# Four expert blocks move from dense matmuls to row gathers in a one-core decoder step

## The chip, the cores and the metric

The kernel runs on one core of one Trainium2 chip. A time is device microseconds of one execution of the whole program. Times of the kernel before, three runs: 3084.05, 3080.38 and 3078.86 us, so a median of 3080.38 us.

## The reference

The program is one layer of a decoder trunk for 512 prompt tokens and 64 sample tokens, with a model width of 2048. A modulation, a combined input projection, two recurrent and convolutional head groups and an output projection come first; they are not touched here. Then comes a mixture of 16384 single-neuron experts (cut to what matters):

```python
q = (xb @ w_q).reshape(PEER_BLOCK, PEER_HEADS, 2, HALF_DIM)          # 8 heads, two halves
sc = jnp.einsum('thpk,pnk->thpn', q, sub_keys)                       # 128 keys in each half
v1, i1 = lax.top_k(sc[:, :, 0], 16)
v2, i2 = lax.top_k(sc[:, :, 1], 16)
...                                                                  # top 16 of the sums
eidx = i1 * 128 + i2                                                 # 128 picks a token
g = softmax(top)
act = gelu(einsum('td,thkd->thk', xb, expert_u[eidx])) * g
out = einsum('thk,thkd->td', act, expert_v[eidx])
x = x + gate2 * out ;  y = rmsnorm(x, final_g)
```

So each token picks 128 of the 16384 experts, takes the product of its 2048-wide row with each picked row of `expert_u`, and sums the picked rows of `expert_v` with the results as weights.

## The kernel before, in words

The 16384 experts are 128 blocks of 128, a block being all experts with the same first key. At run time the kernel counts how often each first key is picked and sorts the blocks by it. The first `L` blocks (80) are computed **densely**: every prompt token against all 128 experts of the block on TensorE, in three matmuls per product (high and low parts of the fp32 operands), and the result is multiplied with a matrix of weights that is zero where nothing was picked. The picks of prompt tokens that fall in the other 48 blocks, and all picks of the sample tokens, are **gathered**: an indirect DMA issued by GpSimd brings up to 128 rows of 2048 floats (one for each partition, 1.05 MB if all are there), and VectorE takes the dot product (line 1577) or adds the scaled row to a sum (line 1605). One such gather is a **slot**. Prompt tokens are sorted by how many picks they have outside the dense blocks, and cut into five groups. `SORTED` gives for each group its first token, its size and its number of slots; in the two groups of 64 tokens a token has two partitions, so its room is twice the slots. The numbers of slots are fixed when the program is built; a partition with no pick left brings no row, but VectorE works through the whole slot all the same. If a token had more picks than room, a slow second path at the end of the program would run.

The sample tokens (slot group 0) have 64 slots, the five prompt groups have 37, 23, 40, 33 and 26, together 159. Each slot is used twice, once for u and once for v.

The stages that matter, in order of time:

- until 1127 us: projections, heads, queries and scores.
- **The U stage**, 1127 to 2120 us: 160 pieces. A piece is half a dense block of `expert_u`: SP loads 512 KB (`raw`), ScalarE makes its high part (`xhi`, line 1203), GpSimd its low part (`xlo`, line 1204), and TensorE runs 24 matmuls (line 1713). Two pieces end in an activation (`act`, line 1716) that goes to DRAM (`actd`). Between the pieces VectorE chooses and sorts, later builds the weight matrix (`op` and `wr`, line 1922; small matmuls on line 1936; `gd` in DRAM), and uses the u slots. Gathers go into a ring of five row buffers here, and at most four are fetched ahead.
- **The V stage**, 2120 to 3053 us: 80 steps of two pieces each. A step multiplies four dense blocks with a quarter of the 2048 columns: 48 matmuls (line 1736). The blocks are taken in groups of eight (two steps for each quarter) and at the end of four; after each group's quarter VectorE adds the four banks to `acc` (line 1765). For each four blocks, GpSimd loads the activations (`actr`) and the weights (`gsb`) back, VectorE multiplies them (`weigh`) and ScalarE and VectorE split the product (`halve`: `ahi` on line 1683, `alo` on line 1687). The v slots run beside it, with seven row buffers; their order is group 0, 3, 1, 2, 4, 5. The sum of a finished group is scattered to DRAM (`accd`).
- the end: the last group of dense blocks, the scattered sums added by TensorE (`tok`), the sample tokens' own finish (`finish_b`), the final norm and the stores of `y`.

Each engine runs its instructions in the order in which the program issues them, and that order is written out by hand. In the U stage a loop over pieces decides before each piece how many slots to use: at fixed rates while the slots are still being chosen, and after the last choice evenly over the pieces that are left, so that at the end of the stage all u slots and the first ten v slots have been used (`gather_to` with `NU + EARLY_V`, `E0 = NU2 - 14`). The weight matrix is spread over the pieces up to `E0 - 6`. In the V stage a table of room per step sets when each slot is used. On GpSimd one queue holds the `xlo` of the dense pieces, the gathers, the loads of `actr` and `gsb`, the stores of `gd` and the scatters. A gather waits there until its row buffer has been used by VectorE, and everything behind it waits too.

Of the kernel before, what the change touches and what calls it, by code (L numbers as in the profile page):

```python
# [33 lines left out]
L = 80  # L34
SG = 4
GROUPS = (8,) * 9 + (4, 4)
# [5 lines left out]
SORTED = ((0, 64, 37), (64, 64, 23), (128, 128, 40), (256, 128, 33), (384, 128, 26))  # L42
# [40 lines left out]
def build(ctx, tc, A, O, dbg=None):  # L83
# [1503 lines left out]
    def gather_v(i):  # L1587
# [7 lines left out]
        def add(j):  # L1595
# [22 lines left out]
            for o in range(0, 128, n):  # L1618
                after.append([gu[0] + 2 + 4 * (o > 0), lambda o=o: out(o)])
            after.append([gu[0] + 2 + 4 * (128 // n), lambda: row_log.__setitem__(a, True)])  # L1620
# [57 lines left out]
    def halve(sg, part):  # L1678

        if part == 0:  # L1680
            pool = ep if sg % 3 < 2 else pools["vx"]
            hi, lo = (pool.tile([128, SG, NA], F32R, name=f"{x}{sg}", tag=f"{x}{sg % 3}", bufs=1) for x in ("ahi", "alo"))
            S.activation(hi, acts[sg], AF.Copy)
            ahg[sg] = (hi, lo)
            return
        hi, lo = ahg[sg]
        V.tensor_sub(lo, acts.pop(sg), r32(hi))  # L1687
        for j in range(SG):
            ahl[SG * sg + j] = (hi[:, j, :], lo[:, j, :])
# [101 lines left out]
    def token_norm(sq, n, nm, pool, banks):  # L1791
# [12 lines left out]
        if nm == "a":  # L1804
            V.tensor_copy(R, pr[:, :n])
        else:
            S.activation(R, pr[:, :n], AF.Copy)
# [131 lines left out]
    def g_out(b, pg):  # L1939
# [5 lines left out]
        if b0 == TC // 4 - 1:  # L1945
            full = stg.pop(c)
            for q in range(0, L, L // 4):
                puts.append(lambda q=q: G.dma_start(
                    gd[q // SG:(q + L // 4) // SG, :, c, :].rearrange("s p x -> p s x"),
                    full[:, q:q + L // 4, :].rearrange("p (s i) t -> p s (i t)", i=SG)))  # L1950
# [31 lines left out]
    for n in range(NU2):  # L1982
# [61 lines left out]
        if n - E0 == 2:  # L2044
            load_group(0)
        for sg, o in ((0, 3), (1, 7)):
            if n - E0 == o:
                load_weights(sg)
        if n - E0 == 6:
            weigh(0)  # L2050
        if n - E0 == 7:
            halve(0, 0)
        if n - E0 == 8:
# [4 lines left out]
        if n == NU2 - 1:  # L2058
            weigh_kept(2)
    hp_.close()  # L2060
# [13 lines left out]
    jobs[0] = [lambda: weigh_kept(3)]  # L2074
    jobs[1] = [lambda: halve(1, 0)]
    jobs[2] = [lambda: halve(1, 1)]
    for sg in range(2, L // SG):
# [7 lines left out]
        jobs.setdefault(h_, []).append(lambda sg=sg: halve(sg, 0))  # L2085
        jobs.setdefault(h_ + 2, []).append(lambda sg=sg: halve(sg, 1))
# [206 lines left out]
```

## Time and profile before

| what | value |
|---|---|
| median of three runs | 3080.38 us |
| the profiled execution | 3082.9 us, span 3081.0 us |
| granted TensorE clock, mean over the span | 0.987 |
| U stage, first to last of its matmuls | 1127.4 to 2120.1 us |
| V stage, first to last of its dense matmuls | 2120.1 to 3052.7 us |
| TensorE, VectorE, ScalarE, GpSimd busy | 97%, 72%, 34%, 57% |
| DMA, mean over the span | 286 GB/s |

The share of busy time of TensorE counts each matmul from its start to its modelled end, and matmuls overlap. The rows of windows therefore give a number in brackets behind the busy time, which is how many instructions fall into the window; the time between two starts is read from it. In a window's row the last three numbers are the granted clock, the mean busy share of the 16 DMA engines, and the GB/s that they moved.

### The profile page before, as it was taken

To read this page: it belongs to the slowest core of one execution; us is meant where nothing else is said; L and a number is where in the kernel's file an instruction comes from. 1 tells how busy PE (TensorE), PEld (TensorE's weight loads), DVE (VectorE), ACT (ScalarE), POOL (GpSimd) and SP (SyncE) were. 2 spreads that over 40 slices of the span, in tenths; PEclk is the share of its full clock that TensorE was granted. 3 is DMA by queue.
4 is the path that set the end of the run, shared out by engine and by line. 5 is a ranking of instruction groups with operands and counts; after the bars stand their busy time and mean duration, and the time that the engine had idled before them with its cause. 6 is when DMAs were issued, how large, how long until landed. Compare 5 with 4: busy or idle time off the path is not lost. (4 is left out here: it accounts for less than half of the span.)

```text
span 3081.0 us, 49243 instructions
## 1 busy us (share of the span) xinstructions
PE 2985.7 (97%) x18521; PEld 2546.5 (83%) x18521; DVE 2222.8 (72%) x3422; ACT 1051.4 (34%) x1675; POOL 1757.3 (57%) x1071
## 2 busy tenths in 40 slices
PE   6999999999999999999999999999999999989996
PEld 4788888899999998878888888877888878878775
DVE  6465532153366899988899999867788798798875
ACT  3344311232253232224655655532322222222222
POOL 2233333344313336666677777777787787876851
PEclk9999999999999999999999999999999999999998
DMA  9743566644432238999879999999999998999973
GB/s 400 295 153 135 177 217 212 212 163 146 132 120 91 74 99 291 315 350 382 318 285 396 384 407 358 383 379 382 377 409 411 410 373 299 361 373 395 382 261 131
DMA packets 238901, 880.90 MB, mean 286 GB/s; under 512 B 36246, under 2 KB 37142, under 8 KB 178102
## 3 DMA queue, kind: packets, MB, share of 16 engines
q0 software_dynamic: 78096, 475.29, 38.8%
q1 hardware_dynamic: 148896, 381.17, 35.0%
q10 hardware_dynamic: 11664, 21.24, 1.8%
q8 instruction: 146, 2.39, 0.3%
q14 instruction: 99, 0.81, 0.1%
HBM read 878.84 MB, written 65.76 MB: 307 GB/s over the span
## 5 line engine op out<-in xcount | busy, mean ns | idle before, releaser
L1204 POOL TENSOR_TENSOR xlo<-raw,xhi 128x1024 fp32r<-128x1024 f32 x320 | 800.4, 2510 | 273.2 <-ACT xhi L1203 270.1
L1203 ACT ACTIVATE xhi<-raw 128x1024 fp32r<-128x1024 f32 x320 | 338.4, 1061 | 789.1 <-PE pv L1736 365.1
L1577 DVE SCALAR_TENSOR_TENSOR u<-u,hT 128x2048 f32<-128x2048 f32 x223 | 504.4, 2282 | 99.0 <-DMA u<-u,rows 98.7
L1605 DVE SCALAR_TENSOR_TENSOR accB<-v,dots,accB 128x2048 f32<-128x2048 f32 x211 | 496.2, 2352 | 108.1 <-DMA v<-v,rows 106.0
L1736 PE MATMUL pv<-ahi,xhi 128*128 128x512 f32 x1280 | 504.6, 394 | 18.1 <-ACT xhi L1203 12.5
L1713 PE MATMUL pu<-hhi,xhi 128*128 128x512 f32 x1280 | 507.0, 396 | 0.7 <-ACT qt L1229 0.7
L1736 PE MATMUL pv<-alo,xhi 128*128 128x512 f32 x1280 | 502.5, 393 | 2.3 <-DVE alo L1687 2.3
L1713 PE MATMUL pu<-hhi,xlo 128*128 128x512 f32 x1280 | 499.0, 390 | 5.7 <-POOL xlo L1204 5.7
L1736 PE MATMUL pv<-ahi,xlo 128*128 128x512 f32 x1280 | 502.0, 392 | 0.0
L1713 PE MATMUL pu<-hlo,xhi 128*128 128x512 f32 x1280 | 499.4, 390 | 0.0
L1549 POOL DMA_INDIRECT u<-u,rows x223 | 226.8, 1017 | 166.2 <-DVE u L1577 124.1
L1736 PEld LDWEIGHTS pv<-ahi,xhi 128*128 128x128 f32 x1280 | 243.1, 190 | 73.0 <-ACT xhi L1203 15.6
L1713 PEld LDWEIGHTS pu<-hhi,xlo 128*128 128x128 f32 x1280 | 240.7, 188 | 57.4 <-POOL xlo L1204 6.6
L1713 PEld LDWEIGHTS pu<-hhi,xhi 128*128 128x128 f32 x1280 | 240.6, 188 | 56.4 <-issue 1.7
L1736 PEld LDWEIGHTS pv<-alo,xhi 128*128 128x128 f32 x1280 | 243.0, 190 | 52.7 <-DVE alo L1687 2.6
L1736 PEld LDWEIGHTS pv<-ahi,xlo 128*128 128x128 f32 x1280 | 242.8, 190 | 51.2 <-POOL xlo L1204 0.2
L1713 PEld LDWEIGHTS pu<-hlo,xhi 128*128 128x128 f32 x1280 | 240.7, 188 | 47.3
L1549 POOL DMA_INDIRECT v<-v,rows x223 | 244.5, 1096 | 60.5 <-issue 39.1
L873 POOL TENSOR_TENSOR wlo_q<-raw_q,whi_q 128x1024 fp32r<-128x1024 f32 x30 | 73.3, 2443 | 175.3 <-ACT whi_q L872 113.4
L1930 ACT ACTIVATE op<-op,it 128x128 f32<-128x128 f32 x512 | 155.2, 389 | 0.0
L1716 ACT ACTIVATE act<-pu 128x512 f32<-128x512 f32 x80 | 47.9, 599 | 297.9 <-PE pu L1713 285.6
L138 POOL TENSOR_TENSOR wlo_o<-raw_o,whi_o 128x1024 fp32r<-128x1024 f32 x31 | 75.1, 2423 | 112.0 <-ACT whi_o L136 108.5
(570 smaller groups left out, 5610.4 us busy)
## 6 DMA issues: line engine op xcount, KB each, us to landing
wa<-w_ada SPq DMA_DIRECT2D x96, 1024.0 KB, 7.2
raw<-ut SPq DMA_DIRECT2D x160, 512.0 KB, 7.8
raw<-vq SPq DMA_DIRECT2D x320, 256.0 KB, 14.9
gd<-stg POOLq DMA_DIRECT2D x64, 320.0 KB, 12.0
gsb<-gd POOLq DMA_DIRECT2D x20, 1024.0 KB, 11.4
actd<-act ACTq DMA_DIRECT2D x76, 256.0 KB, 7.8
actr<-actd POOLq DMA_DIRECT2D x19, 1024.0 KB, 12.0
raw_o<-w_out SPq DMA_DIRECT2D x32, 512.0 KB, 3.7
```

Of the source, the lines that this page charges most:

```text
L138: lo_engine(share).tensor_sub(lo, raw, r32(hi))
L873: G.tensor_sub(lo, qraw.pop(j), r32(hi))
L1203: S.activation(hi, raw, AF.Copy)
L1204: G.tensor_sub(lo, raw, r32(hi))
L1549: G.indirect_dma_start(out=out, out_offset=None, in_=src, in_offset=bass.IndirectOffsetOnAxis(ap=idx, axis=0), bounds_check=NE * 128 - 1, ...
L1577: V.scalar_tensor_tensor(r, r, 1.0, st["h"], op0=ALU.mult, op1=ALU.mult, accum_out=dots[i][:, j:j + 1])
L1605: V.scalar_tensor_tensor(st["a"], r, dots[i][:, j:j + 1], st["a"], op0=ALU.mult, op1=ALU.add)
L1713: PE.matmul(pu, st[:, kk, :], movA[mv](k), start=k == 0 and a == 0, stop=k == KD - 1 and a == 2)
L1716: S.activation(act, pu, AF.Gelu_apprx_tanh)
L1736: PE.matmul(pv, st, mv, start=first and j == 0 and a == 0, stop=last and not (end and k >= LATE_K) and j == SG - 1 and a == 2)
L1930: S.activation(ops[:, j0 + j, :], ops[:, j0 + j, :], AF.Copy, scale=it[2][:, b * 4 + j:b * 4 + j + 1])
```

## The change

`L` becomes 76: four blocks of 128 experts fewer are computed densely, so the U stage has 152 pieces, and the V stage 76 steps, with one group of four blocks at its end in place of two. The picks that fell into those four blocks are now gathered. The slots become 36, 25, 44, 36 and 29, together 170. The store of the weight matrix is cut into parts of 20 blocks, the last part being smaller. The other edits move work or give it to another engine:

- the scatter of a finished group is issued two uses of a slot later, and its buffer is released one use later;
- the second group of four blocks is split in two parts (`halve(1, ..)`): the first three blocks are split from their own call, the first half of it before the V stage begins;
- the first loads of `actr` and `gsb`, their product and their split move three to four pieces later behind `E0`; in the V stage the split of each later group moves one or two quarter steps later;
- the six points at which the sample tokens' finish goes on (`fplan`) are spread over the last steps in another way;
- the copy of the final norm's factors goes from VectorE to ScalarE, and three of the last stores of `y` go from SP's queue to ScalarE's.

```diff
-L = 80
+L = 76
-GROUPS = (8,) * 9 + (4, 4)
+GROUPS = (8,) * 9 + (4,)
-SORTED = ((0, 64, 37), (64, 64, 23), (128, 128, 40), (256, 128, 33), (384, 128, 26))
+SORTED = ((0, 64, 36), (64, 64, 25), (128, 128, 44), (256, 128, 36), (384, 128, 29))
...
-                after.append([gu[0] + 2 + 4 * (o > 0), lambda o=o: out(o)])
-            after.append([gu[0] + 2 + 4 * (128 // n), lambda: row_log.__setitem__(a, True)])
+                after.append([gu[0] + 4 + 4 * (o > 0), lambda o=o: out(o)])
+            after.append([gu[0] + 3 + 4 * (128 // n), lambda: row_log.__setitem__(a, True)])
...
-    def halve(sg, part):
+    def halve(sg, part, a=0, b=SG):
+        if sg not in ahg:
+            pool = ep if sg % 3 < 2 else pools["vx"]
+            ahg[sg] = [pool.tile([128, SG, NA], F32R, name=f"{x}{sg}", tag=f"{x}{sg % 3}", bufs=1) for x in ("ahi", "alo")]
+        hi, lo = (x[:, a:b, :] for x in ahg[sg])
...
+            S.activation(hi, acts[sg][:, a:b, :], AF.Copy)
...
+        V.tensor_sub(lo, acts[sg][:, a:b, :], r32(hi))
...
-        if nm == "a":
-            V.tensor_copy(R, pr[:, :n])
-        else:
-            S.activation(R, pr[:, :n], AF.Copy)
+        S.activation(R, pr[:, :n], AF.Copy)
...
-        if n - E0 == 2:
+        if n - E0 == 5:
             load_group(0)
-        for sg, o in ((0, 3), (1, 7)):
+        for sg, o in ((0, 5), (1, 10)):
             if n - E0 == o:
                 load_weights(sg)
-        if n - E0 == 6:
+        if n - E0 == 8:
             weigh(0)
-        if n - E0 == 7:
+        if n - E0 == 10:
             halve(0, 0)
-        if n - E0 == 8:
+        if n - E0 == 11:
             halve(0, 1)
...
             weigh_kept(2)
+            halve(1, 0, 0, 3)
...
-    jobs[0] = [lambda: weigh_kept(3)]
-    jobs[1] = [lambda: halve(1, 0)]
-    jobs[2] = [lambda: halve(1, 1)]
+    jobs[0] = [lambda: weigh_kept(3), lambda: halve(1, 1, 0, 3)]
+    jobs[1] = [lambda: halve(1, 0, 3)]
+    jobs[2] = [lambda: halve(1, 1, 3)]
...
-        jobs.setdefault(h_, []).append(lambda sg=sg: halve(sg, 0))
-        jobs.setdefault(h_ + 2, []).append(lambda sg=sg: halve(sg, 1))
+        jobs.setdefault(h_ + 2, []).append(lambda sg=sg: halve(sg, 0))
+        jobs.setdefault(h_ + 3, []).append(lambda sg=sg: halve(sg, 1))
...
-    fplan = {(last, 3), (last + 1, 0), (last + 1, 2), (last + 2, 0), (last + 2, 1), (last + 2, 3)}
+    fplan = {(last, 1), (last + 1, 1), (last + 1, 3), (last + 2, 0), (last + 2, 2), (last + 3, 0)}
...
-            nc.sync.dma_start(O["y"][:, k, :NA], ak)
+            (nc.scalar if order.index(k) in (3, 8, 12) else nc.sync).dma_start(O["y"][:, k, :NA], ak)
```

Two places show how this moves the instructions. The first is GpSimd's queue in the last twenty pieces of the U stage. A row `xlo` is one dense piece, `u_N` is the gather of u slot N of a group, `h2r` fetches a group's token rows, and `gd` stores a part of the weight matrix. Before:

```order
L1204 TENSOR_TENSOR xlo_20265<-raw_20190,xhi_20264 128x1024
L1948 DMA gd<-stg_19883 128x5x128
L1549 DMA u_4_20297<-u,rows_9005 128x2048
L1549 DMA u_5_20302<-u,rows_9005 128x2048
L1204 TENSOR_TENSOR xlo_20340<-raw_20259,xhi_20339 128x1024
```

With the change:

```order
L1204 TENSOR_TENSOR xlo_20201<-raw_20118,xhi_20200 128x1024
L1549 DMA u_29_20223<-u,rows_9003 128x2048
L1549 DMA u_30_20228<-u,rows_9003 128x2048
L1549 DMA u_31_20233<-u,rows_9003 128x2048
L1549 DMA u_32_20238<-u,rows_9003 128x2048
L1204 TENSOR_TENSOR xlo_20276<-raw_20195,xhi_20275 128x1024
L1946 DMA gd<-stg_20019 128x5x128
L1549 DMA u_33_20280<-u,rows_9003 128x2048
L1549 DMA u_34_20285<-u,rows_9003 128x2048
L1549 DMA u_35_20290<-u,rows_9003 128x2048
L1558 DMA h2r_20295<-h2d,tok 128x2048
L1204 TENSOR_TENSOR xlo_20329<-raw_20270,xhi_20328 128x1024
```

Where two gathers stood between two dense pieces, three or four stand now. Counted over the last twenty pieces of the stage (from one `xlo` to the next), 34 row fetches were issued before and 59 are issued now; in the pieces ahead of the last twenty-four the counts per ten pieces are the same to within four.

The second place is the same queue in the V stage, in the middle of the sample tokens' slots. A `v_N` is the gather of a v slot, and two `xlo` in a row are one step. Before:

```order
L1204 TENSOR_TENSOR xlo_22387<-raw_22121,xhi_22386 128x1024
L1204 TENSOR_TENSOR xlo_22391<-raw_22207,xhi_22390 128x1024
L1549 DMA v_41_22425<-v,rows_8995 128x2048
L1660 DMA gsb_22433<-gd 128x2048
L1549 DMA v_42_22461<-v,rows_8995 128x2048
L1204 TENSOR_TENSOR xlo_22481<-raw_22216,xhi_22480 128x1024
L1204 TENSOR_TENSOR xlo_22485<-raw_22295,xhi_22484 128x1024
```

With the change:

```order
L1204 TENSOR_TENSOR xlo_22180<-raw_21913,xhi_22179 128x1024
L1204 TENSOR_TENSOR xlo_22184<-raw_22000,xhi_22183 128x1024
L1549 DMA v_43_22205<-v,rows_8995 128x2048
L1549 DMA v_44_22223<-v,rows_8995 128x2048
L1660 DMA gsb_22228<-gd 128x2048
L1549 DMA v_45_22256<-v,rows_8995 128x2048
L1204 TENSOR_TENSOR xlo_22278<-raw_22009,xhi_22277 128x1024
L1204 TENSOR_TENSOR xlo_22282<-raw_22093,xhi_22281 128x1024
```

Between two steps two or three gathers stood, 11 for each four steps; now there are three, 12 for each four steps in full slots, and up to 15 where the slots of a group run empty.

More of the change, by code (lines that the diff above doesn't have):

```diff
@@ L1676, in weigh_kept @@
                         g[:, :, j * TC:(j + 1) * TC], op=ALU.mult)
-    def halve(sg, part):
+    def halve(sg, part, a=0, b=SG):
[3 more added lines that the diff above has]
+        hi, lo = (x[:, a:b, :] for x in ahg[sg])
         if part == 0:
[L1681 to L1684, printed above, removed]
+            S.activation(hi, acts[sg][:, a:b, :], AF.Copy)
             return
[L1686 to L1689, printed above, removed]
+        V.tensor_sub(lo, acts[sg][:, a:b, :], r32(hi))
+        for j in range(a, b):
+            ahl[SG * sg + j] = (hi[:, j - a, :], lo[:, j - a, :])
     ahg = {}
@@ L1946, in g_out @@
             full = stg.pop(c)
[L1947 to L1950, printed above, removed]
+            for q in range(0, L, 20):
+                e = min(q + 20, L)
+                puts.append(lambda q=q, e=e: G.dma_start(
+                    gd[q // SG:e // SG, :, c, :].rearrange("s p x -> p s x"),
+                    full[:, q:e, :].rearrange("p (s i) t -> p s (i t)", i=SG)))
     def put(n):
```

## The prediction

> **What bounds the kernel now.** I read the page's shares first, then the V stage in windows, then who waited for whom.
>
> ```profile
> PE 2985.7 (97%) x18521; PEld 2546.5 (83%) x18521; DVE 2222.8 (72%) x3422; ACT 1051.4 (34%) x1675; POOL 1757.3 (57%) x1071
> L1736 PE MATMUL pv<-ahi,xhi 128*128 128x512 f32 x1280 | 504.6, 394 | 18.1 <-ACT xhi L1203 12.5
> 1900.00:2000.00 100.00, 100.00 (x723) 81.33 (x722) 85.24 (x79) 59.58 (x133) 75.67 (x56) 1.00 0.98 391
> 2200.00:2300.00 100.00, 100.00 (x443) 82.84 (x442) 80.30 (x45) 27.40 (x26) 79.64 (x49) 1.00 1.02 410
> 2300.00:2400.00 100.00, 100.00 (x443) 82.84 (x442) 84.29 (x49) 23.82 (x23) 79.79 (x50) 1.00 1.02 411
> 2500.00:2600.00 100.00, 95.61 (x410) 78.06 (x409) 89.93 (x52) 20.48 (x18) 76.41 (x49) 0.97 0.91 339
> 2700.00:2800.00 100.00, 91.80 (x398) 75.28 (x397) 85.92 (x50) 23.46 (x21) 75.11 (x48) 0.97 0.98 380
> ```
>
> TensorE is busy, but its mean of 394 ns is not its pace: in the window from 2200 us 443 matmuls start in 100 us, one each 0.226 us. A block costs 96 matmuls (48 for u, 48 for v), so 21.7 us of TensorE and not the 38 us that 394 ns would give. The same windows show the second limit: DMA at a share of 1.02 and 410 to 411 GB/s while TensorE runs without a gap. Both are full there. Where TensorE does lose time, it waits for what DMA brings late:
>
> ```profile
> PE pv L1736 <- ACT xhi L1203: 12.5, 3, 6.9
> PE pu L1713 <- POOL xlo L1204: 5.7, 2, 3.5
> PE ph L1823 <- DMA tokb<-accs: 4.3, 1, 4.3
> PE pv L1736 <- DVE alo L1687: 2.3, 1, 2.3
> PE ph L1802 <- DVE rcfb L159: 2.3, 1, 2.3
> PE pv L1736 <- ACT ahi L1683: 1.6, 1, 1.6
> DVE accB L1605 <- DMA v<-v,rows: 100.1, 66, 5.0
> POOL u L1549 <- DVE u L1577: 108.7, 74, 4.6
> ```
>
> The first six rows are TensorE's own waits. The last two, VectorE's from 2120 to 3000 us and GpSimd's from 1400 to 2120 us, are the reserve: 100 us of waiting for v rows and 109 us for a free row buffer, little of which reached TensorE. So the kernel runs at TensorE's pace with DMA just able to follow, and the change takes from the first and gives to the second.
>
> **What the change removes.** 4 blocks x 96 matmuls x 0.226 us = 86.8 us of TensorE, 43.4 in each stage. The small matmuls of the weight matrix stay in number. DMA loses, with the sizes of these rows, 4 x (2 x 0.524 + 4 x 0.262) = 8.4 MB of dense rows and about 4 MB of `actd`, `actr`, `gd` and `gsb`:
>
> ```profile
> raw<-ut SPq DMA_DIRECT2D x160, 512.0 KB, 7.8
> raw<-vq SPq DMA_DIRECT2D x320, 256.0 KB, 14.9
> actd<-act ACTq DMA_DIRECT2D x76, 256.0 KB, 7.8
> gd<-stg POOLq DMA_DIRECT2D x64, 320.0 KB, 12.0
> gsb<-gd POOLq DMA_DIRECT2D x20, 1024.0 KB, 11.4
> actr<-actd POOLq DMA_DIRECT2D x19, 1024.0 KB, 12.0
> q0 software_dynamic: 78096, 475.29, 38.8%
> ```
>
> **What it adds.** Slots are not bytes, since empty places bring no row. Following the reference's routing on its inputs, 16261 picks of the prompt tokens lie outside the first 80 blocks, and 18378 outside the first 76. With 8192 of the sample tokens, at 8192 bytes and twice (u and v), that is 400.6 MB before; with the other transfers of GpSimd's queue (`gsb`, `actr`, `gd`, token rows, scatters) it makes 475 MB, the last row above. The change therefore adds 2117 x 8192 B = 17.3 MB to each stage, and net some 11 MB to each. By the same count no token has more picks than room, so the second path stays unused.
>
> VectorE gets 11 slots more of each kind:
>
> ```profile
> L1577 DVE SCALAR_TENSOR_TENSOR u<-u,hT 128x2048 f32<-128x2048 f32 x223 | 504.4, 2282 | 99.0 <-DMA u<-u,rows 98.7
> L1605 DVE SCALAR_TENSOR_TENSOR accB<-v,dots,accB 128x2048 f32<-128x2048 f32 x211 | 496.2, 2352 | 108.1 <-DMA v<-v,rows 106.0
> L1765 DVE TENSOR_TENSOR acc<-acc,pv 128x512 f32<-128x512 f32 x144 | 96.6, 680 | 39.6 <-PE pv L1736 39.6
> L1687 DVE TENSOR_TENSOR alo<-actr,ahi 128x2048 fp32r<-128x2048 f32 x20 | 61.2, 3060 | 5.1 <-ACT ahi L1683 5.1
> L1665 DVE TENSOR_TENSOR actr<-actr,gsb 128x2048 f32<-128x2048 f32 x19 | 58.2, 3063 | 0.0
> ```
>
> 11 x 2.28 = 25 us in U; in V 11 x 2.35 = 26 us less 16 additions of 0.68 us (one group of blocks fewer) and 6 us for one `weigh` and `alo`, so 9 us. VectorE has that much room on average (90% and less in the windows above), DMA has not.
>
> **The end of the U stage.** The slots are spread evenly only after the last choice, so all the added u slots fall into the last pieces: 59 row fetches in the last twenty pieces where 34 were. With the filling of each slot they carry 50.9 MB, and the twenty pieces bring 13.1 MB of `raw` and `act` and 6 MB of `gd`, `gsb` and `actr`: 70 MB. The old last twenty moved 49 MB between these two activations (the tile row's last start is the last of them):
>
> ```profile
> 1999.35 0.60 ACT L1716 ACTIVATE act<-pu 128x512 f32<-128x512 f32 x1 [2.60 <-PE pu L1713]
> L1716 ACT ACTIVATE act<-pu x80: 597/598/604, 1143.5 to 2122.7; 128x512 f32<-128x512 f32 x80
> ```
>
> That is 123 us at 397 GB/s. At 411 GB/s 70 MB need 171 us. A second floor is the ring: four fetches ahead of the one in use, each some 13.2 us to landing:
>
> ```profile
> u<-u,rows POOLq DMA_INDIRECT x223, 13.2
> L1549 POOL DMA_INDIRECT u<-u,rows x223 | 226.8, 1017 | 166.2 <-DVE u L1577 124.1
> 1350.00:1375.00 25.00, 22.26 (x98) 16.71 (x96) 18.74 (x26) 5.92 (x7) 19.85 (x13) 1.00 1.02 421
> ```
>
> With 2.3 us of use and 1 us of issue a buffer turns in 16.5 us, five of them give one slot each 3.3 us, and 59 slots take 195 us. The last row shows a stretch in which this ring did keep DMA full, at 421 GB/s, so the value lies near the DMA floor. I take 175 us: +52, from +42 (165 us, at 425 GB/s) to +72. Against the 43.4 saved the U stage gains nothing: **+9 us**, from -1 to +29. The 5.7 us that GpSimd, with `xlo` behind it, stood at the first `actr` load until the last `gd` was stored lie inside the 123 us; the load comes three pieces later now, and the wait goes:
>
> ```profile
> POOL actr L1655 <- DMA gd<-stg: 5.7, 1, 5.7
> ```
>
> **The V stage.** Four steps at TensorE's pace are 192 x 0.226 = 43.4 us. Before, 11 full slots (11.5 MB), eight pieces (4.2) and one `gsb` and one `actr` (2.1) make 17.8 MB: 410 GB/s, which is the windows' own rate. Now 12 slots make 18.9 MB: at 411 GB/s 45.9 us, 2.5 us late each four steps. Where the slots are thin, 15 of them cost VectorE 15 x 2.35 plus about 11 us of other work, 46 us, also late. I added up for each stretch of four steps what the largest of the three needs (bytes over 411 GB/s, VectorE, TensorE) exceeds TensorE's: 21 us before and 48 now. Taken over two or eight steps it is 41 to 64, and 12 to 30. The stage lost 36 us in fact: from the first weights of the stage to the matmul `ph`, 2120.1 to 2981.1 us, are 76 steps, 861 us, against 76 x 48 x 0.226 = 825.
>
> ```profile
> L1736 PEld LDWEIGHTS pv<-ahi,xhi x1280: 186/188/333, 2120.1 to 3052.0; 128*128 128x128 f32 x183
> 2981.10 7.06 PE ph L1823 x32
> 2980.00:3000.00 20.00, 18.90 (x75) 16.61 (x76) 9.03 (x10) 1.10 (x2) 1.55 (x1) 0.68 0.94 352
> 3065.63 6.67 DVE acc L2155 x10
> ```
>
> So the sum sees the right size, and I add its growth, 23 us (18 to 27; none if the seven row buffers even everything out, 45 if each late gather stops TensorE through VectorE's order): **-20 us**, from -43 to +2.
>
> **The edits around it.** Splitting group 1 early removes the 2.3 and 1.6 us at the start of V, unless VectorE comes late from the U stage with `alo` behind it: -4 to +6, taken as -3. Moving `fplan` gives the sample rows 10.9 us instead of 2.7 before their matmul and the norm more matmuls to hide behind: the 4.3 and 2.3 us go, and with them some of the 6 us that the clock of 0.68 cost after the wait: -6, from 0 to -12. Their load waits behind the same dense loads in SP's queue, so no more than that. Later loads of `actr` and `gsb` take GpSimd's wait away but not the bytes; later scatters and later splits move work within full queues; the copy on ScalarE and three stores on its queue are under 1 us at the end, where VectorE's ten products set the pace (6.67 us, the row from the chain of waits).
>
> **The sum**, on the profiled execution's 3082.9 us: +9 - 20 - 3 - 6 = -20, so 3063 us; that execution lies 2.5 us above the median of the runs, so 3060 us.
>
> The Trainium skill ("DMA: Bandwidth & Descriptors", Specifications) puts the ceiling of the 16 engines at 435 GB/s; by it, as an estimate, the 70 MB would take 161 us and the sum would be 14 us lower. No window of 100 us in the trace of before comes above 411.
>
> **Rivals.**
> - *DMA has room.* A share of 1.02 at 411 GB/s could be demand, not ceiling: it is exactly what four steps ask for. With 425 GB/s the U end adds 42 us, and V's growth falls to 10: -1 - 33 - 9 = -43, 3037 us; with all of it hidden, 3080 - 87 - 9 = 2984. For it: 421 GB/s in one 25 us stretch, and the windows from 2200 to 2400 us without any stall. Against it: VectorE's 100 us of waiting for rows at that rate.
> - *The ring of five binds (slower).* At the end of U GpSimd stands at a gather whose buffer VectorE has not used, and the next `xlo` stands behind it. This row says 31.85 / 2.28 = 14 slots in 50 us, 3.6 us each, beside a full DMA:
>
> ```profile
> 1900.00:1950.00 50.00, 31.85 (x27) 1.00 1.02 417
> ```
>
>   59 slots then take 211 us, +88 instead of +52, and V begins with VectorE behind: U +45, V -15, the rest -3: 3107 us. It decides against the change from 3.3 us a slot if the rest gives its 29 us (123 + 43 + 29 = 195 us for 59), and from 2.8 us if the rest gives nothing. Against it: thin slots land sooner, and that pace was asked for by the program.
> - *It cancels.* The U end at its ring floor, 195 us, and V and the edits as forecast: 3080 + 29 - 29. The mean landing of 13.2 us speaks for it, the stretch at 421 GB/s against it.
>
> **How the numbers follow.** Forecast 0.50, DMA has room 0.20, the ring 0.20, cancelling 0.10. A measurement of this kernel cannot tell less than 0.2%, 6 us. Faster: the first two but for a twentieth of the forecast, 0.68; same: 0.12; slower: 0.20. The likeliest alone spans 3035 to 3078; the range reaches to 3012 in the first rival and to 3102 in the second.
>
> **What would show it.** The last u dot should come with TensorE waiting on `xlo` for some 40 to 60 us in the last twenty pieces, where it waited 5.7, at 400 GB/s or more. Until then the U stage should match before, piece for piece. V should be some 20 us shorter, with DMA shares at 1.0 nearly throughout and more waits on `acc`, `xhi` or `alo`. If DMA moves 425 GB/s over 100 us, the first rival is right; if the U end runs below 390 GB/s with GpSimd waiting on VectorE, the second.

## The result, and the profile after

The changed kernel takes 3106.74 us (median of four runs, 3104.25 to 3112.58), the kernel before 3080.68 us beside it: ratio 1.0089, 95% interval 1.0077 to 1.0101. It is 27 us slower, where 20 us faster was forecast, and lies 5 us outside the range.

Four marks divide the span of the profiled executions: the first matmul of U (line 1713), the first product of V (line 1736), the first copy of a bank into `acc` (line 1763) and the first sum of the last group (line 1767).

| stretch, us | before | after | difference | forecast |
|---|---|---|---|---|
| until U | 1127.4 | 1129.2 | +1.8 | 0 |
| U | 992.9 | 1003.6 | +10.7 | +9 |
| start of V, to the first copy into `acc` | 20.3 | 33.3 | +13.0 | -3 |
| main part of V | 852.7 | 844.8 | -7.9 | -20 |
| last group to the end | 87.7 | 95.0 | +7.3 | -6 |
| span | 3081.0 | 3105.9 | +24.9 | -20 |

From the page of the kernel after, the shares, four groups (name, count, busy time and mean ns, idle time just before and its releaser) and the queue that carries the gathers (packets, MB, share):

```profile
PE 2942.7 (95%) x18137; PEld 2483.6 (80%) x18137; DVE 2246.6 (72%) x3446; ACT 1031.1 (33%) x1656; POOL 1731.6 (56%) x1075
q0 software_dynamic: 80720, 506.82, 40.7%
L1605 DVE SCALAR_TENSOR_TENSOR accB<-v,dots,accB 128x2048 f32<-128x2048 f32 x222 | 522.3, 2353 | 138.0 <-DMA v<-v,rows 134.2
L1577 DVE SCALAR_TENSOR_TENSOR u<-u,hT 128x2048 f32<-128x2048 f32 x234 | 530.0, 2283 | 110.2 <-DMA u<-u,rows 105.6
L1736 PE MATMUL pv<-ahi,xhi 128*128 128x512 f32 x1216 | 488.9, 402 | 39.3 <-DVE acc L1765 21.0
L1713 PE MATMUL pu<-hhi,xlo 128*128 128x512 f32 x1216 | 481.6, 396 | 41.6 <-POOL xlo L1204 41.6
```

GpSimd's queue carries 31.5 MB more (506.82 against 475.29): the 34.7 MB of added rows less three megabytes of `gd`, `gsb` and `actr`. TensorE's idle time stands in two places, at `xlo` in U (41.6 us) and in V. The windows of the two kernels, cut at the last twenty pieces of U, the first product of V and the first sum of the last group (us, busy time and count of each engine, granted clock, DMA share, GB/s); first before, then after, with four stretches of 100 us out of V:

```profile
2000.00:2120.00 120.00, 114.26 (x572) 93.36 (x572) 84.34 (x66) 36.74 (x53) 89.03 (x63) 0.99 0.95 377
2120.00:2993.00 873.00, 848.31 (x3695) 698.72 (x3694) 713.34 (x413) 208.90 (x196) 662.42 (x411) 0.98 0.96 371
```

```profile
1957.00:2133.00 176.00, 134.40 (x610) 104.59 (x608) 134.70 (x115) 38.74 (x56) 112.50 (x88) 0.87 0.92 368
2133.00:3011.00 878.00, 826.72 (x3468) 662.07 (x3467) 727.29 (x411) 197.52 (x187) 645.77 (x416) 0.97 0.98 383
2200.00:2300.00 100.00, 100.00 (x434) 81.00 (x433) 79.70 (x38) 28.35 (x29) 82.57 (x53) 1.00 1.01 407
2300.00:2400.00 100.00, 97.36 (x423) 79.03 (x422) 80.52 (x49) 21.91 (x20) 74.96 (x50) 1.00 1.02 413
2700.00:2800.00 100.00, 88.45 (x368) 70.69 (x367) 80.65 (x48) 19.53 (x18) 70.32 (x49) 0.95 0.99 380
2800.00:2900.00 100.00, 94.59 (x393) 74.86 (x392) 82.43 (x47) 20.92 (x19) 73.97 (x48) 0.97 0.98 384
```

Two things are to be seen. V has four steps fewer ahead of its last group and is 5 us longer (878 against 873): 324 MB at 371 GB/s became 336 MB at 383. And in the window from 2200 us, in which TensorE never waits and its clock is 1.00, it starts 434 matmuls where it started 443 before. The forecast had TensorE at 0.226 us a matmul throughout. The granted clock follows TensorE's waits: 1.00 from 2200 us, where it has none, and 0.95 from 2700 us, where it is busy for 88.45 of 100 us. So a part of what V loses stands beside its waits as slower matmuls; no run takes the two apart.

### The profile page after: what moved, and what is told of

It reads as the page before. It is cut to its first block, busy times and chain, and to the rows that moved or that the text cites. A ratio compares the mean times of both kernels' runs of the same rounds, so it can differ in the third digit from the quotient of the medians.

```text
span 3105.9 us, 48371 instructions
## 1 busy us (share of the span) xinstructions
PE 2942.7 (95%) x18137; PEld 2483.6 (80%) x18137; DVE 2246.6 (72%) x3446; ACT 1031.1 (33%) x1656; POOL 1731.6 (56%) x1075
## 3 DMA queue, kind: packets, MB, share of 16 engines
q0 software_dynamic: 80720, 506.82, 40.7%
q1 hardware_dynamic: 145008, 372.00, 33.8%
## 5 line engine op out<-in xcount | busy, mean ns | idle before, releaser
L1204 POOL TENSOR_TENSOR xlo<-raw,xhi 128x1024 fp32r<-128x1024 f32 x304 | 743.8, 2454 | 298.3 <-ACT xhi L1203 289.5
L1605 DVE SCALAR_TENSOR_TENSOR accB<-v,dots,accB 128x2048 f32<-128x2048 f32 x222 | 522.3, 2353 | 138.0 <-DMA v<-v,rows 134.2
L1577 DVE SCALAR_TENSOR_TENSOR u<-u,hT 128x2048 f32<-128x2048 f32 x234 | 530.0, 2283 | 110.2 <-DMA u<-u,rows 105.6
L1203 ACT ACTIVATE xhi<-raw 128x1024 fp32r<-128x1024 f32 x304 | 321.3, 1060 | 791.7 <-PE pv L1736 288.4
L1736 PE MATMUL pv<-ahi,xhi 128*128 128x512 f32 x1216 | 488.9, 402 | 39.3 <-DVE acc L1765 21.0
L1713 PE MATMUL pu<-hhi,xlo 128*128 128x512 f32 x1216 | 481.6, 396 | 41.6 <-POOL xlo L1204 41.6
L1713 PE MATMUL pu<-hhi,xhi 128*128 128x512 f32 x1216 | 489.3, 402 | 2.0 <-ACT stg L1940 1.3
L1736 PE MATMUL pv<-alo,xhi 128*128 128x512 f32 x1216 | 486.4, 400 | 4.0 <-DVE alo L1687 4.0
L1713 PE MATMUL pu<-hlo,xhi 128*128 128x512 f32 x1216 | 480.9, 395 | 0.0
L1549 POOL DMA_INDIRECT v<-v,rows x234 | 267.8, 1144 | 98.3 <-issue 42.3
L1736 PEld LDWEIGHTS pv<-ahi,xhi 128*128 128x128 f32 x1216 | 233.4, 192 | 100.2 <-issue 20.2
L1713 PEld LDWEIGHTS pu<-hhi,xlo 128*128 128x128 f32 x1216 | 232.1, 191 | 97.7 <-POOL xlo L1204 47.2
```

What stands on the lines that cost most here:

```text
L1203: S.activation(hi, raw, AF.Copy)
L1204: G.tensor_sub(lo, raw, r32(hi))
L1549: G.indirect_dma_start(out=out, out_offset=None, in_=src, in_offset=bass.IndirectOffsetOnAxis(ap=idx, axis=0), bounds_check=NE * 128 - 1, ...
L1577: V.scalar_tensor_tensor(r, r, 1.0, st["h"], op0=ALU.mult, op1=ALU.mult, accum_out=dots[i][:, j:j + 1])
L1605: V.scalar_tensor_tensor(st["a"], r, dots[i][:, j:j + 1], st["a"], op0=ALU.mult, op1=ALU.add)
L1713: PE.matmul(pu, st[:, kk, :], movA[mv](k), start=k == 0 and a == 0, stop=k == KD - 1 and a == 2)
```

## The experiments

Theories on the table: **A, placement** (the changed tables ahead of them move five of the seven row buffers, the third weight buffer, `actr`, `gsb` and the `ahi` and `alo` of two groups in three from 224 to 160 bytes behind a multiple of 256 in their partition, as the built programs place them, and this slows the products); **B, DMA's bytes** are what the stages wait for; **C, the slots as such** (VectorE's work and order, the ring of buffers); **D, the side edits**. The column "against before" is the ratio less 1, times 3080 us.

| run | ratio (95%) | against before | U | start | main | end |
|---|---|---|---|---|---|---|
| after | 1.0089 (1.0077-1.0101) | +27 | 1003.6 | 33.3 | 844.8 | 95.0 |
| e1 after, old places | 1.0084 (1.0068-1.0101) | +26 | 1000.0 | 33.8 | 845.0 | 95.0 |
| e2 before, new places | 1.0036 (1.0020-1.0051) | +11 | 996.4 | 19.3 | 857.7 | 84.2 |
| e3 after, rows as many as before | 1.0000 (0.9991-1.0010) | 0 | 996.2 | 31.8 | 822.7 | 95.2 |
| e4 edits alone, 80 blocks | 0.9972 (0.9963-0.9982) | -9 | 989.4 | 19.7 | 836.6 | 96.0 |
| e5 after, half the last u rows | 0.9989 (0.9976-1.0002) | -3 | 972.6 | 32.2 | 843.8 | 95.2 |
| e6 e4, old norm steps | 0.9985 (0.9974-0.9996) | -5 | 993.1 | 17.8 | 847.9 | 84.5 |
| e7 e4, old scatters | 0.9985 (0.9975-0.9994) | -5 | 989.9 | 19.6 | 839.5 | 93.6 |
| e8 e1 and e3 together | 0.9988 (0.9978-0.9998) | -4 | 997.1 | 32.1 | 820.6 | 95.0 |
| e9 e1, half the prompt's v rows | 0.9894 (0.9878-0.9911) | -33 | 1004.0 | 33.7 | 785.9 | 92.5 |
| e10 e1, no weighings | 1.0087 (1.0070-1.0103) | +27 | 1003.4 | 33.4 | 844.4 | 95.6 |
| e11 after, two early v slots | 1.0064 (1.0047-1.0081) | +20 | 985.9 | 27.9 | 860.1 | 98.2 |
| e12 e4, weighing earlier | 0.9974 (0.9964-0.9984) | -8 | 990.9 | 20.2 | 837.4 | 94.3 |
| e13 before, end's edits | 0.9999 (0.9990-1.0009) | 0 | 993.7 | 22.3 | 839.3 | 98.1 |
| e14 before, split edits | 0.9988 (0.9976-1.0001) | -4 | 988.4 | 20.6 | 850.9 | 87.9 |
| e15 after, kept weighings first | 1.0097 (1.0076-1.0119) | +30 | 1003.0 | 34.7 | 845.0 | 94.8 |
| e16 e4, kept weighings first | 0.9979 (0.9970-0.9988) | -6 | 993.3 | 21.4 | 835.0 | 93.7 |
| e17 after, places at 0 | 1.0074 (1.0057-1.0091) | +23 | 1003.9 | 32.2 | 836.1 | 97.7 |
| e18 e4, places at 192 | 1.0027 (1.0016-1.0039) | +8 | 995.7 | 21.4 | 843.9 | 96.0 |

**e1 and e2: the places put back, and the places changed alone.** `shift_l` is a tile that no instruction uses; its length only moves the tiles behind it.

```diff
-    actp.tile([128, 24], F32, name="shift_l", bufs=1)
+    actp.tile([128, 40], F32, name="shift_l", bufs=1)     # in e1; in e2, on the kernel before: [128, 8]
```

> The kernel after, with one pad of 24 words made 40 words, so that the row buffers, the third weight buffer, ahi and alo start at the same place modulo 256 bytes as in the kernel before (the change made tiles ahead of them 192 bytes longer). Nothing else differs. Theory A, placement: the products pv in V run 2.9% slower in the kernel after (0.2333 us apart instead of 0.2268 in the first group, 434 to 436 in 100 us instead of 443) because of where those tiles now lie. Then 443 in 100 us come back, and the time falls by 12 to 22 us, to 3085 to 3095 us. Theory B, the full DMA (or VectorE) slows the products and placement does nothing: 434 to 436 stay and the time is 3107 within 4 us. Between them, the pace comes back but DMA takes the gain as waits on acc and xhi: 443 in windows without waits, 3098 to 3105 us.

> The kernel before, with the same pad made 8 words instead of 24, so that those tiles start where they start in the kernel after, modulo 256 bytes. Theory A, placement: V's products fall from 443 to 434 to 436 in 100 us, and the time rises by 12 to 24 us, to 3093 to 3105 us. Theory B: 443 stays and the time is 3081 within 4 us.

The same stretch of V in e1, then in e2:

```profile
2200.00:2300.00 100.00, 100.00 (x443) 82.84 (x442) 76.94 (x39) 27.16 (x28) 82.47 (x53) 1.00 1.02 409
2127.00:3006.00 879.00, 814.63 (x3472) 662.15 (x3470) 728.79 (x410) 197.36 (x187) 646.08 (x417) 0.97 0.97 382
```

```profile
2200.00:2300.00 100.00, 100.00 (x434) 81.07 (x433) 79.04 (x42) 26.10 (x26) 78.40 (x48) 1.00 1.02 412
```

Nothing but the places differs, and both ways the pace follows them: 443 with the old, 434 with the new. A is shown as a cause of the pace. But e1 is no faster than the kernel after (+26 against +27), with the same 879 us for V at 382 GB/s. The gain of the pace went into TensorE's waits, here those of e1 (us in total, times, longest):

```profile
PE pv L1736 <- DVE acc L1765: 22.4, 13, 8.4
PE pv L1736 <- ACT xhi L1203: 19.2, 5, 7.9
PE pv L1736 <- DVE alo L1687: 7.8, 4, 3.6
PE pv L1736 <- DVE accB L1605: 5.5, 1, 5.5
```

The kernel after has 21.0, 14.7 and 4.0 us in the first three and nothing in the fourth; at `xlo` it has 7.8, e1 5.4. In e2, whose rows and blocks are those of the kernel before, the slow products cost 11 us.

**e3 and e8: the added rows left out.**

```diff
-                             bounds_check=NE * 128 - 1, oob_is_err=False)
+                             bounds_check=14863, oob_is_err=False)
```

> The kernel after, with the bound of the gathers lowered from row 16383 to row 14863: picks of rows above it bring nothing, so about 2117 rows fewer come in each stage, as many as the change added (17.3 MB in each stage). All instructions stay, and the picks above the bound use what the buffer held, so this part of the sum is left out. Theory B, DMA's bytes set the time: the last twenty pieces of U, 175 us, fall by 35 to 42 us, the start of V loses most of its 13 us, V's main part falls by 10 to 25 us; 3030 to 3060 us in all. Theory C, the number of slots through the five buffers and VectorE's order set it, bytes do not: the twenty pieces fall by less than 12 us and the time by less than 25 us, 3082 to 3105 us. The slower products (theory A) stay in either case.

> The kernel after with both edits of the first set: the tiles placed as before (which gave 2 us by itself) and about 2117 rows fewer in each stage (which gave 28 us by itself; that part of the sum is left out). If DMA takes up what the faster products give, as the waits on acc and xhi in the aligned kernel say, the two together give more than their sum: V at 0.2268 us a product with DMA relieved, 3057 to 3067 us. If the 28 us came from elsewhere and placement is worth 2 us in any case: 3074 to 3079 us. The number of slots alone (VectorE, 11 more) is then what is left against the edits alone less eight blocks: 3071 - 87 = 2984 us plus the U stage's loss.

With all 170 slots but only as many rows as the kernel before brings, the time falls by 27 us, to that of the kernel before; main part and end of V give 22 of them. The last twenty pieces of U fell by 7 us only, not by 35 to 42: that expectation was wrong in itself, since the bound takes 8% of the rows everywhere, and of the 51 MB at the end of U that is 4 MB, 10 us at 411 GB/s. So e3 says B for V and nothing on U. e8, with the old places too, is 4 us below e3, inside what the two intervals leave open; V's main part went from 822.7 to 820.6. The expected 12 us and more did not come.

**e5: half of the last u rows.**

```diff
-            take(held[j][0], A["u"], rows_i[i][:, j:j + 1])
+            take(held[j][0], A["u"], rows_i[i][:, j:j + 1], 8191 if gf[0] >= NU - 49 else NE * 128 - 1)
```

Here and in e9 `take` gets the bound of the gather as an argument of its own (cut).

> The kernel after, with the last 48 u slots fetching only the rows below 8192, about half of them: some 19 MB of the 70 MB in the last twenty pieces of U stay away (that part of the sum is left out), every instruction stays. DMA as the bound there: 51 MB at 411 GB/s are 124 us, VectorE then limits with 59 slots of 2.3 us, so the twenty pieces fall from 175 to 135 to 145 us, the 33 us from the first product of V to its first sum fall towards 20, and the time falls by 30 to 50 us, to 3055 to 3075 us. Slots as the bound (five buffers, VectorE's order): the pieces stay above 160 us, the start of V above 30, and the time falls by less than 15 us.

```profile
1957.00:2102.00 145.00, 127.87 (x617) 100.97 (x615) 133.81 (x116) 38.15 (x56) 114.09 (x89) 0.93 0.86 308
```

The twenty pieces take 145 us instead of 176, with as many VectorE instructions (116, and 115 in the row of the kernel after), and the whole time falls by 31 us. So the rows set the time at the end of U, and the slots' work on VectorE does not: the 59 slots go through five buffers in 2.5 us each as soon as their rows are thinner. How the rows do it is not told apart. Thinner rows are fewer bytes, but they also land sooner (a median of 6.6 us for a u gather in this window, 13.2 in the U stage before), and so the ring of five turns faster too. At 145 us VectorE is close behind with 133.81 us busy. What did not move is the start of V, 32.2 us.

**e9 and e10: half the v rows of the prompt groups, or a fifteenth of VectorE's work in V.**

```diff
-            take(held[j][0], A["v"], rows_i[i][:, j:j + 1])
+            take(held[j][0], A["v"], rows_i[i][:, j:j + 1], 8191 if i else NE * 128 - 1)     # e9
...
+        if sg >= 2:                                                                           # e10, in weigh
+            gsb.pop(sg)
+            return
         V.tensor_tensor(a, a, gsb.pop(sg).rearrange("p c (i t) -> p i c t", t=TC), op=ALU.mult)
```

> The aligned kernel after (3104 us), with the v rows of groups 1 to 5 fetched only below row 8192, about half of them, some 75 MB less in V (that part of the sum is left out); every instruction stays. In the traces VectorE waits 132 us for v rows in the main part of V. If those rows are late because DMA is full, the waits go and V runs at TensorE's pace: from the first product of V to the end 974 us become 905 to 925, 3035 to 3055 us in all. If a slot's row comes late because of the order of work on GpSimd and VectorE, over 90 us of the waits stay and the time stays above 3080 us.

> The aligned kernel after (3104 us), without the 17 weighings in V (the product of the activations with the weight matrix is left out from the third group on, so their part of the sum is wrong by that factor). VectorE loses 17 x 2.9 = 50 us of work; every transfer and every product of TensorE stays. If VectorE bounds V (its work and its waits for rows fill 790 of 790 us in the trace, its waits for TensorE fell from 35 us before to 2), the time falls by 25 to 50 us, to 3054 to 3079 us. If DMA's bytes bound V, it falls by less than 10 us, 3094 to 3104 us.

V from its first product to the last group's first sum, and VectorE's row of the page, for e1 (the row of the page alone), then in e9, then in e10:

```profile
L1605 DVE SCALAR_TENSOR_TENSOR accB<-v,dots,accB 128x2048 f32<-128x2048 f32 x222 | 522.3, 2353 | 145.3 <-DMA v<-v,rows 138.8
```

```profile
2129.00:2949.00 820.00, 798.13 (x3470) 654.11 (x3468) 730.41 (x411) 198.15 (x187) 658.31 (x416) 0.99 0.88 318
L1605 DVE SCALAR_TENSOR_TENSOR accB<-v,dots,accB 128x2048 f32<-128x2048 f32 x222 | 522.0, 2352 | 64.8 <-DMA v<-v,rows 57.5
```

```profile
2131.00:3009.00 878.00, 815.99 (x3489) 663.93 (x3488) 680.74 (x394) 197.08 (x187) 631.90 (x416) 0.97 0.98 383
L1605 DVE SCALAR_TENSOR_TENSOR accB<-v,dots,accB 128x2048 f32<-128x2048 f32 x222 | 522.5, 2354 | 194.2 <-DMA v<-v,rows 191.2
```

This is the plainest pair. Taking the bytes away gives 59 us and brings TensorE near its pace: 72 steps of 48 matmuls at 0.2267 us are 783 of the 820 us, and the start, longer by 13 us, is among the rest. GpSimd had no less to do (658.31 us, 646.08 in e1). Taking 48 us of VectorE's work away (728.79 to 680.74) gives nothing: V takes 878 us where it took 879, and the wait for v rows grows in VectorE's place, from 138.8 to 191.2 us. V of the changed kernel is bound by DMA. VectorE only looked bound, because its work and its wait for rows filled the time together.

**e11: fewer v slots ahead of V.**

```diff
-EARLY_V = 10
+EARLY_V = 2
```

> The kernel after (3107 us), with 2 instead of 10 v slots done ahead within the U stage: 8 full slots (8.4 MB, 20 us of DMA at 411 GB/s, 18 us of VectorE) leave the last pieces of U and come in V. If both stages are bound by what the slots cost, the time only moves: the U stage 20 to 25 us shorter, V as much longer, 3100 to 3112 us. If the crowded end costs something of its own (33 us from the first product of V to its first sum, where 20 were), that goes: 3090 to 3098 us.

U becomes 17.7 us shorter, the start 5.4, main part and end 18.5 longer. Most of the time moved, as both B and C have it; the 7 us between +27 and +20 are at the edge of the intervals.

**e4, e13, e14: the side edits.** e4 is the changed kernel with `L`, `GROUPS` and `SORTED` of the kernel before. e13 puts only the end's edits into the kernel before, e14 only the split and the later loads:

```diff
-    fplan = {(last, 3), (last + 1, 0), (last + 1, 2), (last + 2, 0), (last + 2, 1), (last + 2, 3)}
+    fplan = {(last, 1), (last + 1, 1), (last + 1, 3), (last + 2, 0), (last + 2, 2), (last + 3, 0)}
...
-        jobs.setdefault(h_, []).append(lambda sg=sg: halve(sg, 0))
-        jobs.setdefault(h_ + 2, []).append(lambda sg=sg: halve(sg, 1))
+        jobs.setdefault(h_ + 2, []).append(lambda sg=sg: halve(sg, 0))
+        jobs.setdefault(h_ + 3, []).append(lambda sg=sg: halve(sg, 1))
```

> The kernel before with all of the change but its sizes: 80 blocks and 159 slots stay, with the later scatters, later and split second group, later first loads, later steps of the final norm and the stores on two queues. Tiles lie where they lay before. As forecast: the edits gain 9 us (start of V -3, end -6), 3072 us. The other theory, from the trace of the kernel after (start of V +13, end +7): part of this comes from the edits themselves, so that the time is 3083 to 3095 us. If the start and the end suffer only from the crowded DMA of the new sizes, it is 3072 to 3080 us.

> The kernel before with the end's edits alone: the final norm's steps at the new six places, the copy of R on ScalarE, three of the last stores on ScalarE's queue. The forecast gave them -6 us, between 0 and -12: 3073 us. The other reading, since putting the old places back into the kernel with all edits cost 3 us at the most: -3 to 0 us, 3076 to 3080.

> The kernel before with the second group split in parts, the first loads later and the splits of every group one to two column steps later; scatters and end as before. The forecast gave the start -3 us and the later splits nothing: 3076 us. The other reading, since all edits together shortened V's main part by 16 us while the end grew by 8: -6 to -8 us, 3071 to 3073.

```profile
2117.00:2973.00 856.00, 838.61 (x3660) 690.02 (x3659) 708.65 (x413) 207.97 (x196) 661.71 (x412) 0.99 0.96 374
```

This row is e4's V from its first product to the last group. Together the edits gain 9 us (6 to 11): e4 at 3071.0 us is faster than both kernels. The end's edits alone give nothing (e13). They only move the mark: the main part is 13 us shorter and the end 10 longer, because steps of the sample tokens' norm now stand behind the last group's first sum instead of ahead of it. The split edits alone give 4 us, with an interval that just reaches zero, and not at the start, which stays at 20.6.

**e6 and e7: one edit taken out of e4** (the six places of `fplan`; the scatters two slots earlier again, `gu[0] + 2` for `gu[0] + 4`, and the release of their buffer one slot earlier).

> The kernel with the edits alone (80 blocks, 3071 us), with the steps of the final norm back at the six places where they were before. In the traces the stretch from the first last-group sum to the end took 87.7 us before and 96.0 with the edits, 95.0 in the kernel after. If the moved steps cost that, it falls to 88 to 90 here and the time to 3062 to 3066 us. If V merely ends at another place and the last part is set by what comes before it (late gathers, dense loads), the two parts together stay at 933 us and the time at 3071 within 4 us.

> The kernel with the edits alone (3071 us), with the scatters two slots earlier again, as in the kernel before. The edits shortened V up to the first last-group sum by 16 us (852.7 to 836.6), which the forecast had put at nothing for the scatters. If the later scatters (GpSimd no longer standing at a sum that VectorE has not finished, with gathers and xlo behind it) bring it, 8 to 16 us come back, 3079 to 3086 us. If it comes from the later splits and loads, the time stays at 3071 within 4 us.

Each costs some 4 us of the 9, with overlapping intervals. Main part and end of e6 are 932.4 us together, of e4 932.6: the mark moved back, the sum did not change. Which edit brings how much is not told apart.

**e12, e15, e16: VectorE's and ScalarE's order.** In e12 each weighing comes three column steps earlier (`h_ - 5` for `h_ - 2`, on e4). In e15 (on the kernel after) and e16 (on e4) the first three kept weighings come ahead of the gathers of their piece:

```diff
+            if n == NU2 - 2:
+                weigh_kept(0)
+                weigh_kept(1)
+            if n == NU2 - 1:
+                weigh_kept(2)
             gather_to(G0 + (NU + EARLY_V - G0) * ...
```

> The kernel with the edits alone (80 blocks, 3071 us), with each weighing three column steps (8 us) earlier on VectorE. In its trace ScalarE stands 54 us at ahi for the weighing, ten times, with the next xhi behind it. If that standing reaches TensorE, 4 to 10 us go: 3061 to 3067 us. If xhi is late because the dense rows land late, the time stays at 3071 within 4 us.

> The kernel after (3107 us), with the first three kept weighings ahead of the gathers of their piece instead of behind them on VectorE. In its trace the last activation of U waits 17 us for the second of them, which stands behind three gathered rows. Placing them first should bring that forward by 8 to 10 us, and the 33 us from the first product of V to its first sum to 22 to 26. If that loss stands for itself, the time falls by 6 to 10 us, to 3097 to 3101. If DMA is what V waits for anyhow, V's main part grows by as much, and the time falls by less than 3 us.

> The kernel with the edits alone (3071 us), with the same three weighings first. There the first sum of V comes after 19.7 us, the last activation waits only 5 us for the weighing. Gain 0 to 4 us: 3067 to 3071 us. If more comes, VectorE's order at the start of V counts with the old sizes too.

None gives anything. The waits at the start of V, first in the kernel after, then in e15:

```profile
ACT act L1716 <- DVE actr L1674: 17.0, 1, 17.0
```

```profile
ACT act L1716 <- DVE actr L1674: 8.2, 1, 8.2
PE pv L1736 <- DVE alo L1687: 9.5, 3, 5.7
```

The last activation of U does come sooner, but TensorE then waits 9.5 us for `alo` (2.8 there in the kernel after), and the start stays at 34.7 us. So these weighings are not what makes the start 13 us longer. It is 32 to 35 us in every run with 76 blocks and ten early v slots, with few u rows (e5) or the weighings first, and 27.9 with two early slots (e11). e9 says nothing on it: the first slots of V are the sample tokens', whose rows it left whole. That VectorE comes late out of a U stage with three slots a piece fits this but was not shown.

**e17 and e18: two more places** (pad of 48 words on the kernel after: multiples of 256 bytes; pad of 16 on e4: 192 behind one).

> The kernel after (3107 us), with the pad of 24 words made 48, so that row buffers, third weight buffer, ahi and alo start at multiples of 256 bytes (224 behind one in the aligned kernel, 3104 us; 160 in the kernel after). If DMA moves rows faster to such starts, V's mean of 382 to 383 GB/s rises by 2 to 3% and 15 to 25 us go: 3080 to 3092 us. If it does not care, 3104 to 3107 within 4 us. For the products in the first group of V: 0.2267 us if any place but 160 is good, 0.2325 to 0.2333 or more if 224 is a good place of its own.

> The kernel with the edits alone (3071 us), with the pad of 24 words made 16, so that the same tiles start 192 bytes behind a multiple of 256 (the third group's ahi and alo stay at 224). If the distance of the start to the next multiple of 64 is what counts (224 and 160 both lie 32 behind one, 192 and 0 none), all products of the first groups run alike at some other pace than 0.2267 or 0.2325; if only 160 is bad, 0.2267 and 3071 within 4 us; if 192 is as bad as 160, 0.2325 and 3078 to 3084 us.

Both run the products of the first group at 0.231 to 0.233 us: of the four places only 224 gave 0.2267. e18 is 17 us slower than e4, with nothing else changed. e17 has the slow products too and is yet no slower than e1; V moves faster there:

```profile
2131.00:2999.00 868.00, 825.16 (x3469) 659.87 (x3468) 729.52 (x410) 196.92 (x187) 649.21 (x416) 0.97 0.97 387
```

V takes 868 us at 387 GB/s, against 879 at 382 in e1 and 878 at 383 in the kernel after. The Trainium skill ("DMA: Bandwidth & Descriptors", How a descriptor splits into AXI transactions) says that a transfer that does not start at a multiple of 256 bytes begins at the multiple below, and that the bytes before its start "are fetched but unused and still cost beats", that is, time on the bus. The direction agrees, but no run shows that this is the reason. The 3 us between e17 and e1 are inside the intervals, so a gain of time is not shown.

## Why the prediction was wrong

**The U stage (+9) came out right, in part by luck.** It grew by 10.7 us, the last twenty pieces took 176 us, forecast 175 (190 to the last activation, the forecast's mark, since that one waited 17.0 us for a weighing), and TensorE waited 41.6 us there for `xlo`, forecast 40 to 60. e5 confirms that the rows set the time. But the stretch moved 176 us x 368 GB/s = 65 MB, not 70, and at 368, not at 400 or more: two errors of like size cancelled. Nor was DMA full all through it. Two stretches of 20 us in the kernel after, and GpSimd's longest wait in the twenty pieces:

```profile
2000.00:2020.00 20.00, 10.67 (x36) 7.95 (x35) 17.24 (x15) 2.72 (x3) 12.54 (x11) 0.74 0.82 308
2100.00:2120.00 20.00, 11.61 (x43) 8.83 (x41) 16.89 (x14) 4.40 (x4) 11.16 (x7) 0.83 0.59 211
POOL u L1549 <- DVE u L1577: 48.1, 28, 5.5
```

By the forecast's own sign, below 390 GB/s with GpSimd waiting on VectorE, the end of U is the case of the rival "the ring of five binds". That rival's price was too high, though: 59 slots in 176 us are 3.0 us each, where its floor was 3.3 (195 us) and its row said 3.6. How much of the added time is a full DMA and how much the ring stays open, since e5 relieves both.

**The V stage (-20) is the step that failed**, and in it the growth of DMA's excess over TensorE, put at 23 us. With the edits the same on both sides (e4 to e1) V goes from 856 to 879 us: 43 us of TensorE saved, so 66 lost, the start's 14 among them. The waits grew where the forecast expected them: TensorE's on `acc` rose from 2.7 to 21.0 us in the kernel after. The added bytes were right too (net +11 MB forecast, 336 - 324 = 12 measured). Their price was not. The forecast divided by 411 GB/s, the rate of the first, full slots, and let V lose only where four steps asked for more. V's own mean was 371 GB/s before, at a share of 0.96, and is 383 after, at 0.98; the row quoted from 2700 us already showed 380 at a share of 0.98. At 383 GB/s, the 324 MB of before need 846 of its 873 us, as an estimate. So V was near its DMA bound before, and 43 us less of TensorE bought nothing. e9 and e10 show that bytes and not VectorE do it, outside the start. The Trainium skill's ceiling of 435 GB/s ("DMA: Bandwidth & Descriptors", Specifications), quoted in the forecast, lies farther off still: no 100 us of V in the kernel after came above 413. With that the rival "DMA has room", which asked for 425 over 100 us, is out. (The kernel before did reach 416 GB/s from 1730 to 1830 us, in U; the forecast's 411 holds for V.) The forecast's bound of 45 us for the case that each late gather stops TensorE was the nearer end.

**VectorE's 100 us of waiting for rows were called a reserve.** They were the sign of the bound: e10 took VectorE's work away and the wait took its place; e9 took bytes away and the wait fell from 138.8 to 57.5 us.

**The start (-3)** became +13. e14 gives the split edits 4 us, but not there. The growth comes with the sizes (19.7 in e4, 33.8 in e1). TensorE's waits there are 6.2 us at `xlo`, 3.3 at the last activation, 2.8 at `alo` and 0.8 at `xhi`, where before it had 3.9 in all; what makes these late stays open.

**The end (-6)** became +7.3 by the mark, and nothing in time (e13: -3 to +3 us). The waits named in the forecast did go, 4.3 us at `tokb` and 2.3 at `rcfb`, and a new one of 4.4 us at `sqb` came. That all edits together gave -9 us, as forecast, is no proof of its two terms.

**Not foreseen at all** was that the longer tables move tiles and slow two thirds of V's products, some 72 x 48 x 2/3 x 0.006 = 14 us. In the changed kernel this costs next to nothing, since the gain goes into TensorE's waits (e1), with the old sizes 11 us (e2), and 17 at another place (e18).

The rival "the ring of five binds" named 3107 us, the time that came, but by U +45 and V -15; U was +11 and V, its start included, +5. Its time was right by luck, though its sign at the end of U was met.

## What to carry to other kernels

Price a stage's transfers with the mean rate that this stage reaches at a DMA share near 1, not with the best window of the trace, and when work moves from a compute engine to DMA, first take bytes away by experiment to see whether the engine's saved time can be had at all. An engine whose work and waits for data fill the stage is not itself the bound until taking its work away shortens the stage. After a change of any table's size compare the matmuls per 100 us in a stretch without waits: a change of place alone can slow them.

## What was not expected of the hardware

Places. With a moving operand of 128x512 fp32 and the clock at 1.00, 48 matmuls of V take 10.88 us (0.2267 us each) where the left tiles start 224 bytes behind a multiple of 256, and 11.08 to 11.20 us (0.231 to 0.233) where they start 160, 192 or 0 behind one. In the kernel after, one trace shows both, since every third group's `ahi` and `alo` lie in another pool that kept 224. In this group of eight blocks the third group of four and the fourth alternate step by step; these are the first matmuls of four successive steps:

```profile
2243.22 0.39 PE L1736 MATMUL pv<-ahi,xlo 128*128 128x512 f32 x1
2254.19 0.39 PE L1736 MATMUL pv<-ahi,xlo 128*128 128x512 f32 x1
2265.38 0.40 PE L1736 MATMUL pv<-ahi,xlo 128*128 128x512 f32 x1
2276.39 0.39 PE L1736 MATMUL pv<-ahi,xlo 128*128 128x512 f32 x1
```

10.97, 11.19 and 11.01 us: the steps alternate. This points to the moving operand, but it is not the whole: the third group's steps are not down to 10.88, and in e18 they are slow too at first, 11.12 to 11.15 us, though their `ahi` lies at 224. One of the weight buffers moved as well. Which reads meet each other there stays open. U's moving operand did not move in any of these kernels, and its median matmul stays at 389 ns (min, median, max; first and last start) where V's has 393 in the kernel after, 389 before:

```profile
L1713 PE MATMUL pu<-hhi,xhi x1216: 387/389/632, 1129.2 to 2132.1; 128*128 128x512 f32 x174
L1736 PE MATMUL pv<-ahi,xhi x1216: 387/393/793, 2132.8 to 3077.4; 128*128 128x512 f32 x174
```

DMA's rate in V falls more than its share: 407 to 413 GB/s at 1.01 to 1.02 from 2200 to 2500 us, 380 to 384 at 0.98 to 0.99 from 2700 to 2900, where the slots carry fewer rows. e9 points the same way: with half the prompt's v rows the stage has 318 GB/s at 0.88, against 382 at 0.97. So a share near 1 does not tell the rate at which DMA is full.
